# The ring of operand tiles in a pool of its own, at 4096-byte steps from byte 79,168, and the mLSTM's values in two buffers beside it

## The chip, the core and the metric

The kernel runs on one NeuronCore of a Trainium2 chip. The metric is device time in microseconds (us) of one execution, as the median of several runs. A core has a matrix engine (TensorE, PE in the rows; PEld is its weight load), VectorE (DVE), ScalarE (ACT), GpSimd (POOL) and SyncE (SP), which here issues the DMAs. The engines run on their own instruction streams and meet at semaphores. The on-chip memory SBUF has 128 partitions; an address here is a byte inside a partition, the same in all of them.

## What is computed

The reference runs two blocks of a network one after the other on 256 tokens of width 1024, in fp32. The first has two layers; each is a mixer (mLSTM, dilated attention, gates) and a gated MLP. The second block has two layers too: a windowed attention with 256 context tokens beside the 256 tokens, then a gated linear attention (GLA), each followed by an MLP of hidden width 4096. All weights are read from HBM once.

```python
def first_block(x, c, ...):
    h = layer_norm(x)
    for l in range(2):
        u = h * (1.0 + sc1) + sh1
        y = mixer(u, w_in[l], ...)          # mLSTM, attention, gates: u @ w_in and more
        h = layer_norm(DN_ALPHA * h + g1 * y, ln1_g[l], ln1_b[l])
        u = h * (1.0 + sc2) + sh2
        h = layer_norm(DN_ALPHA * h + g2 * swiglu(u, w1[l], w3[l], w2[l]), ln2_g[l], ln2_b[l])

def channel_mlp(h, w_in, w_out):            # second block
    return jnp.square(jax.nn.relu(h @ w_in)) @ w_out
```

## The kernel before

**Weights.** The weights are packed into 591 tiles of 128x1024 fp32 for the main stream, which `ahead` (L450 and after) keeps moving: SP loads `raw`, ScalarE rounds it to `wh` (L464), VectorE makes the rest `wl = raw - wh`. These tiles lie in the pool `wp`, each at 128 behind a multiple of 256 bytes. A weight tile with the matmuls that use it is called a granule; `gran` (L477) emits one. Each product is made of three TensorE passes, `mm3` (L581): activation-high by `wh`, activation-low by `wh`, activation-high by `wl`.

**Two kinds of product.** In `mm_ws` (L588) the weight slice, 128x128, is loaded as the stationary operand and the activations stream past it, 256 columns at a time (rows `mm<-uT,wh`: first the moving operand, then the stationary one). A granule of this kind has 8 slices of the contraction, k = 0 to 7, and 24 matmuls. In `mm_nat` and the "row" products of the second block the activations are stationary and 512 columns of weight stream (rows `aux<-wh,hid`).

**Where the operands lie.** Activation tiles come from rings. `t4` (L432) hands out tiles of up to 4112 bytes a partition from 27 buffers, in turn; `t2` (L429) tiles of 2048 bytes from 8. Both rings are tags of the one pool `p`. The widest `t4` tile is `v1`, the mLSTM's values with a column of ones, 4x257 fp32, 4112 bytes; the pool rounds that up to 4128. The built program puts the `t4` ring at bytes 78,720 + 4128 n, so the starts of its 27 buffers go through all eight remainders 0, 32, ..., 224 of 256, and the `t2` ring at 202,368 + 2048 n, remainder 128 each. A tile of split activations (`t4x4`, L434) holds two slices k, each with a high and a low part of 1024 bytes, so all its operands have the remainder of its buffer; a granule reads four such tiles. `mlg` (L1097), the hidden activations of the first block's MLP, is a `t2` tile and holds one slice's high and low part.

**What a ring makes wait.** The first write of a tile waits for the last access of the tile that had the buffer before. `order` of the work on each engine is fixed when the program is built: granules follow the list `PLAN`, background generators (`tick`) put other work between them, and VectorE's extra products for the modulation vectors (`ada_step`) are put where a model of TensorE's and VectorE's time (`Core`) has room. The addresses do not enter that model.

Of the kernel before, what the change touches and what calls it, by code (L numbers as in the profile page):

```python
# [9 lines left out]
F32 = mybir.dt.float32  # L10
# [298 lines left out]
class Views(list):  # L309


    def __init__(self, views, pair):
        super().__init__(views)
        self.pair = pair
# [62 lines left out]
class Kernel:  # L377
    LOAD, HI, LO, RAWS = 5, 3, 2, 4

    def __init__(self, ctx, tc, i, o):  # L380
        self.tc, self.nc, self.i, self.o = tc, Core(tc.nc), i, o
        nc = self.nc
        pool = lambda name, bufs, **k: ctx.enter_context(tc.tile_pool(name=name, bufs=bufs, **k))
        self.const = c = pool("const", 1)
        self.wp = pool("wp", 4)
        self.ps = pool("ps", 2, space=PSUM)
        self.p = pool("p", 1)
        self.cur = self.nload = self.nhi = self.nlo = 0
        self.raws, self.hi, self.W = {}, {}, {}
        self.bg, self.deferred = [], []  # L390
        self.filler = iter(())
        self.kv, self.on = [None, None], [None, None]
        self.mix_filler = [self.ctx_qkv, self.ctx_in]
        self.mlp_filler = [self.ctx_out, self.ctx_mlp]
        self.adaq, self.ada_left, self.adaraw = [], {}, {}
        self.room = -250
        self.hold = False
        self.vec = c.tile([128, i["vec"].shape[1]], F32, name="vec")
        self.ident = c.tile([128, 128], F32, name="ident")
        make_identity(tc.nc, self.ident)  # L400
        self.identr = c.tile([128, 128], F32R, name="identr")
        nc.vector.tensor_copy(out=self.identr, in_=self.ident)
        self.ones = c.tile([128, 1], F32, name="ones")
        nc.vector.memset(self.ones, 1.0)
        self.mhalf = c.tile([128, 16], F32, name="mhalf")
        nc.vector.memset(self.mhalf, -0.5)
        self.x = None
# [19 lines left out]
        return self.p.tile([128, 256], F32, tag="t1", name=name, bufs=5)  # L427

    def t2(self, name, shape=(128, 512), dt=F32):  # L429
        return self.p.tile(list(shape), dt, tag="t2", name=name, bufs=8)  # L430

    def t4(self, name, shape, dt=F32):  # L432
        return self.p.tile(list(shape), dt, tag="t4", name=name, bufs=27)

    def t4x4(self, name, n=8):

# [348 lines left out]

    def values(self):

        v1 = [self.t4("v1", (128, 4, 257)) for _ in range(2)]
        for b in range(2):
            self.nc.gpsimd.memset(v1[b][:, :, 256:257], 1.0)  # L790
        return v1
# [1011 lines left out]
    def layer2_attention(self, x, xc):  # L1803
        nc = self.nc
        cols = self.scales(0, "g_pre_mix_2", 0, 1, (0,))
        h = self.next_h(0, x, None, None, cols, lag=2)
        while not h:
            self.tick(False)
            self.fill()
        self.fill(99)  # L1810
        self.hold = False
        h = self.wait(h)
        for cb in (2, 0, 1):
            for _ in self.qkv(0, cb, h, [self.aux(), self.aux()]):
                self.tick(False)
        self.flush()

        self.on[0] = [self.t4("on", (128, 1024)) for _ in range(2)]
        oT = [None] * 8
        pools = (self.aux,) * 4 + (self.trb,)  # L1820
        left = [(0, b, hq) for hq in range(16) for b in range(2)]
        for n, u in enumerate(left):
            self.add(self.unit(pools[n % len(pools)], *u), n)
            if n % 8 == 7:
                self.add(self.o_out(0, n // 8, oT, self.trb), n + 7)
        other = self.mlp_out(1, 1, self.hid_c, self.yc, self.mmb)
        n = 0
        while self.bg:
            n += 1
            self.tick(False)  # L1830
            self.run_deferred()
            if n in (1, 2, 4, 6, 12, 18, 24, 30):
                next(other, None)
            if self.adaq and self.nc.late < self.room:
                self.ada_step()
        self.rest(other)
        gc = self.gain_cols(0, "g_post_mix_2", 2, 0)
        cols = self.scales(0, "g_pre_mlp_2", 3, 4, (0,))
        yl = [[None] * 2 for _ in range(2)]
        for hf in range(2):  # L1840
            banks = [self.aux(), self.aux()]
            for kp in range(4):
                self.gran(("awo", 0, hf, kp), self.mm_nat(kp, self.tokens(oT), banks))
                if hf == 0 and kp == 1:
                    G = self.bcast_cols(gc, "G")
            for b in range(2):
                yl[b][hf] = banks[b]
        ul = self.next_h(0, x, yl, G, cols, lag=2)
        uc = self.uc
        hc = []  # L1850
        for _ in self.mlp_in(2, 1, uc, hc):
            self.tick(False)

        ul = self.wait(ul)
        y = [self.t4("y", (128, 1024)) for _ in range(2)]
        yl = self.halves(y)
        yh = yl + self.yc
        for g in range(3):
            hid = []
            self.rest(self.mlp_in(g, 0, ul, hid))  # L1860
            if g < 2:
                self.rest(self.mlp_out(g, 0, hid, yl, self.aux))
            else:
                self.flush()
                act = lambda k, hl, b: (hid if b < 2 else hc)[k][:, hl, b % 2 * 128:(b % 2 + 1) * 128]
                self.rest(self.mlp_out(g, 2, act, yh, self.aux))
        hid, hc = [], []
        for i in range(8):
            t = self.t4("hid", (128, 2, 512), F32R)
            hid.append(t[:, :, 0:256])  # L1870
            hc.append(t[:, :, 256:512])
            ps = self.mmb()
            self.gran(("mi", 0, 24 + i, 2), self.mm_ws2(ps, [ul, uc]), lambda t=t, ps=ps: self.relu2(ps, t))
        del ul, uc
        self.uc = None
        G = [self.post_gain(0, "g_post_mlp_2", 5, st) for st in range(2)]
        cols = self.scales(1, "g_pre_mix_2", 0, 1, (0, 1))
        self.rest(self.mlp_out(3, 0, hid, yl, self.aux))
        self.h1 = [self.next_h(0, x, yl, G[0], cols, lag=2), None]
        for _ in self.mlp_out(3, 1, hc, self.yc, self.aux):  # L1880
            self.tick(False)
        self.h1[1] = self.next_h(1, xc, self.yc, G[1], cols, lag=2)
        self.h1[0] = self.wait(self.h1[0])
# [19 lines left out]
    def layer2_gla(self, x, xc):  # L1903
        nc = self.nc
# [77 lines left out]
                    yield  # L1982
            ldone.append(1)
        self.add(decay())
        kT = [self.t4("gkT", (128, 2, 512)) for _ in range(2)]
        for hd in range(4):
            ps = self.mmb()
            self.gran(("gk", hd), self.mm_ws2(ps, h), lambda hd=hd, ps=ps: nc.scalar.activation(out=kT[hd // 2][:, hd % 2], in_=ps, func=AF.Copy))
# [144 lines left out]
        for hd in range(4):  # L2133
            if hd == 1:
                self.until(lambda: ldone)
                head(0, 1)
            if hd == 3:
                head(1, 1)
            values(hd)
# [109 lines left out]
```

## Time and profile before

| | us |
|---|---|
| median of 3 runs | 2107.93 (2104.86 to 2108.47) |
| the profiled execution, its time | 2106.81 |
| its span, first to last instruction | 2105.0 |
| PE busy | 2048.7 (97%) |
| PEld busy | 1904.5 (90%) |
| DVE busy | 1587.3 (75%) |
| ACT busy | 1149.7 (55%) |

A busy PE in such a table says only that some matmul was in flight: matmuls overlap each other (a row says 283 ns for one, while the next starts some 118 ns later). What a stream of matmuls costs is read from the distance between their starts, in the timeline. The granted clock of TensorE was 1.00 (its upper level, 2.4 GHz) in nearly the whole span, 0.994 on average.

### The profile page before, as it was taken

Reading aid. Unit: us, or ns where it says so; the run is one execution under the profiler, and the core shown is the slowest. Engines: PE = TensorE matmul, PEld = TensorE weight load, DVE = VectorE, ACT = ScalarE, POOL = GpSimd, SP = SyncE. Lnnn points to the kernel's source line nnn. Section 1 sums busy time; section 2 is a strip of 40 time slices with the busy share of each in tenths; the row PEclk is TensorE's granted clock in tenths of the full one; section 3 lists DMA queues with packets and bytes.
Section 4 is the critical chain, followed back from the end, with each engine's and each line's share of the span. In section 5 each row is a group of like instructions: output and inputs, shape, how many; then the busy total and the mean of one; then the engine's idle time right before and its main releaser. Section 6 shows DMA issues by size and latency. Waiting matters only on the chain.

```text
span 2105.0 us, 38238 instructions
## 1 busy us (share of the span) xinstructions
PE 2048.7 (97%) x15176; PEld 1904.5 (90%) x15176; DVE 1587.3 (75%) x2717; ACT 1149.7 (55%) x1968; POOL 44.4 (2%) x62
## 2 busy tenths in 40 slices
PE   7999999999999999999999999999999999998998
PEld 6999998899998998998999988899998989877997
DVE  7788887698978988998899876777563485466555
ACT  5756665555545656665644455556542464545444
POOL 0000000000000000000000000000000010000000
PEclk9999999999999999999999999999999999999999
DMA  8786566588876786655589855215552352224654
GB/s 336 279 311 215 179 233 215 190 299 305 301 258 207 280 285 227 201 192 189 161 281 352 294 197 180 71 42 179 191 186 95 114 177 86 72 69 145 195 188 134
DMA packets 120884, 426.88 MB, mean 203 GB/s; under 512 B 13664, under 2 KB 18528, under 8 KB 120704
## 3 DMA queue, kind: packets, MB, share of 16 engines
q1 hardware_dynamic: 120704, 424.43, 59.1%
q8 instruction: 119, 1.95, 0.4%
q14 instruction: 61, 0.50, 0.1%
HBM read 423.33 MB, written 1.05 MB: 202 GB/s over the span
## 4 chain that ended last, share of the span: by engine, by line
PE 88%; DVE 6%; ACT 4%; issue 1%; POOL 0%; DMA 0%; DVEq 0%; POOLq 0%; SPq 0%; ACTq 0%
PE mm L338 54%; PE aux L338 28%; PE trb L338 5%; DVE wl L338 1%; ACT wh L464 1%; POOL rs L667 0%; DVE yg L338 0%; ACT xh L1460 0%; DVE mtmp L338 0%; ACT u L896 0%; DVE araw L338 0%; ACT ah L905 0%; DVE ee L338 0%; ACT u L1498 0%; DVE xh L338 0%
## 5 line engine op out<-in xcount | busy, mean ns | idle before, releaser
L338 DVE TENSOR_TENSOR wl<-raw,wh 128x1024 fp32r<-128x1024 f32 x591 | 718.9, 1221 | 165.5 <-PE aux L338 71.1
L464 ACT ACTIVATE wh<-raw 128x1024 fp32r<-128x1024 f32 x591 | 623.6, 1059 | 345.2 <-PE mm L338 121.8
L338 PE MATMUL mm<-uT,wh 128*128 128x256 f32 x3488 | 630.2, 283 | 0.0
L338 PEld LDWEIGHTS mm<-uT,wh 128*128 128x128 f32 x3488 | 535.4, 189 | 2.2 <-ACT va L807 0.4
L338 PE MATMUL mm<-uT,wl 128*128 128x256 f32 x1744 | 488.8, 280 | 0.0
L338 PE MATMUL mm<-hT,wh 128*128 128x256 f32 x1888 | 341.6, 283 | 4.0 <-ACT y L1765 2.1
L338 PEld LDWEIGHTS mm<-uT,wl 128*128 128x128 f32 x1744 | 329.1, 189 | 0.0
L338 PEld LDWEIGHTS mm<-hT,wh 128*128 128x128 f32 x1888 | 293.6, 190 | 10.7 <-ACT y L1765 2.3
L338 PE MATMUL mm<-hT,wl 128*128 128x256 f32 x944 | 265.7, 282 | 0.0
L338 DVE CUSTOM_DVE_ANT_0 araw<-araw,silu 128x1024 f32<-128x1024 f32 x192 | 233.1, 1219 | 7.4 <-DMA araw<-in_w 5.0
L338 PE MATMUL aux<-wh,hid 128*128 128x512 f32 x640 | 199.5, 393 | 0.0
L338 PEld LDWEIGHTS mm<-hT,wl 128*128 128x128 f32 x944 | 178.7, 189 | 0.0
L338 PEld LDWEIGHTS aux<-wh,hid 128*128 128x128 f32 x640 | 117.7, 188 | 24.1
L338 PE MATMUL aux<-mlg,wh 128*128 128x256 f32 x704 | 129.5, 285 | 0.0
L338 DVE TENSOR_TENSOR r<-r 128x256 f32<-128x256 f32 (+1 forms) x88 | 39.4, 448 | 117.5 <-ACT r L1898 117.4
L338 PE MATMUL aux<-wl,hid 128*128 128x512 f32 x320 | 125.4, 392 | 0.0
L338 PEld LDWEIGHTS aux<-mlg,wh 128*128 128x128 f32 x704 | 109.3, 191 | 0.0
L1898 ACT ACTIVATE r<-mm 128x256 f32<-128x256 f32 (+1 forms) x88 | 35.9, 408 | 125.7 <-PE mm L338 125.7
L338 PE MATMUL aux<-mlg,wl 128*128 128x256 f32 x352 | 99.5, 283 | 0.0
L667 POOL TENSOR_TENSOR rs<-ve,mhalf 128x1 f32<-128x1 f32 (+1 forms) x48 | 40.9, 852 | 2043.5 <-DVE ve L338 1858.4
L338 DVE CUSTOM_DVE_ANT_0 junk<-araw,silu 128x1024 bf16<-128x1024 f32 x64 | 77.9, 1217 | 0.0
L338 PE MATMUL mm<-wh,hT 128*128 128x256 f32 (+1 forms) x352 | 77.1, 316 | 0.5 <-DVE qs L338 0.5
(364 smaller groups left out, 3088.1 us busy)
## 6 DMA issues: line engine op xcount, KB each, us to landing
raw<-in_w SPq DMA_DIRECT2D x591, 512.0 KB, 3.9
araw<-in_w SPq DMA_DIRECT2D x192, 512.0 KB, 5.1
abias<-in_abias SPq DMA_DIRECT2D x32, 192.0 KB, 5.5
xc<-in_ctx SPq DMA_DIRECT2D x4, 512.0 KB, 5.9
x<-in_x SPq DMA_DIRECT2D x2, 512.0 KB, 4.2
gb<-in_ln SPq DMA_DIRECT2D x2, 512.0 KB, 6.0
out_x<-x SPq DMA_DIRECT2D x4, 256.0 KB, 2.0
mk<-in_mmask SPq DMA_DIRECT2D x1, 512.0 KB, 5.8
```

What stands on the lines that cost most here:

```text
L338: return f(*a, **k)
L464: nc.scalar.activation(out=wh, in_=self.raws[self.nhi], func=AF.Copy)
L667: nc.gpsimd.tensor_tensor(out=rs, in0=ve, in1=self.mhalf[:, 0:n], op=ALU.pow)
L1898: nc.scalar.activation(out=r[:, 0:n], in_=ps, func=AF.Relu)
```

## The change

Three pools take the place of one. `p4` holds a tile `gap` of 448 bytes and then the `t4` ring, now 25 buffers; `p2` holds the `t2` ring, still 8 buffers; `p` keeps the rest. The three pairs of tiles `v1`, the second block's `on` and `gkT` leave the `t4` ring and take turns in two buffers of a new tag `tv` in `p`. With `v1` gone the widest tile of the `t4` ring has 4096 bytes.

```diff
@@ Kernel.__init__
+        self.p4, self.p2 = pool("p4", 1), pool("p2", 1)
         self.p = pool("p", 1)
+        nc.gpsimd.memset(self.p4.tile([128, 112], F32, name="gap"), 0.0)
@@
     def t2(self, name, shape=(128, 512), dt=F32):
-        return self.p.tile(list(shape), dt, tag="t2", name=name, bufs=8)
+        return self.p2.tile(list(shape), dt, tag="t2", name=name, bufs=8)
     def t4(self, name, shape, dt=F32):
-        return self.p.tile(list(shape), dt, tag="t4", name=name, bufs=27)
+        return self.p4.tile(list(shape), dt, tag="t4", name=name, bufs=25)
+    def tv(self, name, shape):
+        return self.p.tile(list(shape), F32, tag="tv", name=name, bufs=2)
@@ values
-        v1 = [self.t4("v1", (128, 4, 257)) for _ in range(2)]
+        v1 = [self.tv("v1", (128, 4, 257)) for _ in range(2)]
@@
-        self.on[0] = [self.t4("on", (128, 1024)) for _ in range(2)]
+        self.on[0] = [self.tv("on", (128, 1024)) for _ in range(2)]
@@
-        kT = [self.t4("gkT", (128, 2, 512)) for _ in range(2)]
+        kT = [self.tv("gkT", (128, 2, 512)) for _ in range(2)]
```

In the built program the addresses become these (start of a buffer, in bytes of a partition):

| ring | before | after |
|---|---|---|
| `t4` | 78,720 + 4128 n, 27 buffers, remainders of 256: all of 0, 32, ..., 224 | 79,168 + 4096 n, 25 buffers, remainder 64 |
| `t2` | 202,368 + 2048 n, 8 buffers, remainder 128 | 181,568 + 2048 n, 8 buffers, remainder 64 |
| `tv` | in the `t4` ring | 205,024 and 209,152, remainders 224 and 0 |
| weights (`wp`), identity matrix (`const`) | remainder 128; 64 | the same |

The order of the instructions on PE, DVE, ACT and SP is the same in both programs. On POOL one instruction is added, at the start of the program. Before, POOL begins with its constants and then fills the identity matrix `ident`, the padding `pad` and the state `mst`:

```order
L2245 UNCONDITIONAL_BRANCH
masks.py:197 MEMSET ident 128x128
L690 MEMSET pad 128x520
masks.py:199 ISA
masks.py:199 AFFINE_SELECT ident<-ident 128x128
L690 MEMSET pad 128x520
```

After, at the same place:

```order
L2252 UNCONDITIONAL_BRANCH
L390 MEMSET gap 128x112
masks.py:197 MEMSET ident 128x128
L697 MEMSET pad 128x520
masks.py:199 ISA
masks.py:199 AFFINE_SELECT ident<-ident 128x128
```

The fill of `gap` stands ahead of the fill of `ident`; nothing else has moved.

## Rows read from the trace of the kernel before

**Rows 1.** The page: busy time and share by engine; then the chain's shares by engine.

```profile
PE 2048.7 (97%) x15176; PEld 1904.5 (90%) x15176; DVE 1587.3 (75%) x2717; ACT 1149.7 (55%) x1968; POOL 44.4 (2%) x62
...
PE 88%; DVE 6%; ACT 4%; issue 1%; POOL 0%; DMA 0%; DVEq 0%; POOLq 0%; SPq 0%; ACTq 0%
```

**Rows 2.** Groups by shape, PE: line, operation, out<-moving,stationary, xcount | busy, mean ns | idle before.

```profile
L338 PE MATMUL mm<-uT,wh 128*128 128x256 f32 x3488 | 630.2, 283 | 0.0
L338 PE MATMUL mm<-uT,wl 128*128 128x256 f32 x1744 | 488.8, 280 | 0.0
L338 PE MATMUL mm<-hT,wh 128*128 128x256 f32 x1888 | 341.6, 283 | 4.0 <-ACT y L1765 2.1 <-ACT r L1898 1.4 <-DVE hT L338 0.3
L338 PE MATMUL mm<-hT,wl 128*128 128x256 f32 x944 | 265.7, 282 | 0.0
...
L338 PE MATMUL aux<-mlg,wh 128*128 128x256 f32 x704 | 129.5, 285 | 0.0
...
L338 PE MATMUL mm<-mT,wh 128*128 128x256 f32 x256 | 48.9, 291 | 2.6 <-ACT mT L650 1.9 <-DVE mT L338 0.7
L338 PE MATMUL mm<-yat,wh 128*128 128x256 f32 x256 | 46.6, 283 | 0.7 <-DVE yat L338 0.3 <-ACT yat L650 0.3
...
L338 PE MATMUL mm<-ybT,wh 128*128 128x256 f32 x128 | 23.2, 283 | 0.0
```

**Rows 3.** Timeline, PE, a granule of `uT`: start us, length us, operation, xcount.

```profile
708.60 0.40 PE L338 MATMUL mm<-uT,wh 128*128 128x256 f32 x2
...
709.30 0.39 PE L338 MATMUL mm<-uT,wh 128*128 128x256 f32 x2
...
709.98 0.40 PE L338 MATMUL mm<-uT,wh 128*128 128x256 f32 x2
...
710.68 0.39 PE L338 MATMUL mm<-uT,wh 128*128 128x256 f32 x2
...
711.39 0.40 PE L338 MATMUL mm<-uT,wh 128*128 128x256 f32 x2
```

**Rows 4.** Timeline, PE, a granule of `mlg` at slices k = 3 and k = 7.

```profile
454.63 0.40 PE L338 MATMUL aux<-mlg,wh 128*128 128x256 f32 x2
...
456.07 0.40 PE L338 MATMUL aux<-mlg,wh 128*128 128x256 f32 x2
```

**Rows 5.** Timeline, PE: 512-column products, stationary at remainder 128, then at 64.

```profile
1498.56 0.62 PE L338 MATMUL aux<-wh,hid 128*128 128x512 f32 x2
...
1499.92 0.62 PE L338 MATMUL aux<-wh,hid 128*128 128x512 f32 x2
...
1583.34 0.62 PE L338 MATMUL aux<-wh,hid 128*128 128x512 f32 x2
...
1584.71 0.62 PE L338 MATMUL aux<-wh,hid 128*128 128x512 f32 x2
```

**Rows 6.** Windows: stretch, its us, busy us of each engine (instructions), PEclk, DMA share, GB/s.

```profile
421.00:474.00 53.00, 53.00 (x454) 53.00 (x453) 49.15 (x90) 28.91 (x63) 0.00 (x0) 1.00 0.89 299
...
684.00:737.00 53.00, 52.55 (x385) 49.12 (x384) 50.76 (x70) 35.21 (x46) 0.00 (x0) 1.00 0.79 280
```

**Rows 7.** Waits: engine, line, waited for: us in total, times, longest us.

```profile
PE mm L338 <- DVE wl L338: 4.0, 2, 2.4
...
POOL v L790 <- PE mm L338: 12.1, 2, 9.6
```

**Rows 8.** Timeline: the last PE reader of an `hT` tile, and VectorE's first `qT` write.

```profile
1313.16 0.39 PE L338 MATMUL aux<-wl,hT 128*128 128x512 f32 x1
...
1320.75 0.68 DVE L338 CAST qT<-trb 128x512 fp32r<-128x512 f32 x1
```

**Rows 9.** Timeline, POOL and PE, start of the program.

```profile
0.73 0.20 POOL masks.py:197 MEMSET ident<- 128x128 f32 x1 [0.29 <-POOLq L2242]
...
3.47 1.94 PE L338 MATMUL trb<-ident,silu 128*128 128x128 f32 x8 [3.47 <-DVE silu L338]
```

## The prediction

> **What bounds the kernel now.** I read the page first: PE is busy for 97% of the span and makes 88% of the chain of work that ended last [rows 1]. A busy PE need not be a fast PE, so the second view is that of the waits: those of PE are few, the longest kind between weights and PE being 4.0 us in all [rows 7]. So TensorE streams nearly all the time, and what decides is the distance from the start of one matmul to the start of the next. The third view, the groups by shape, says which matmuls there are: 256 activation columns moving past a weight slice [rows 2]. By `mm3` there is one `wl` pass to two `wh` passes, so the five families there hold 3488 + 1744 (`uT`), 1888 + 944 (`hT`), 704 + 352 (`mlg`), 256 + 128 (`mT`), 256 + 128 (`yat`), and with 128 + 64 of `ybT` that is 10,080 matmuls. At some 118 ns each they take 1190 us, over half of the span.
>
> The fourth view, the timeline of single granules, is where the change bites, because the distance depends on the remainder of the moving operand's address by 256. The granule of `uT` at 708.6 us reads four tiles of two slices, six matmuls each; in the built program these lie at the remainders 64, 64, 160 and 128. Their starts are 0.70, 0.68, 0.70 and 0.71 us apart [rows 3]: per matmul 117, 113, 117 and 118 ns, in one granule, with the same weight tile and the same engines busy beside it. `mlg`, at remainder 128 in all its granules, takes 1.44 us for twelve: 120.0 ns [rows 4].
>
> I then paired every matmul of the trace with its instruction in the program, in order, and averaged the distances below 160 ns by the remainder of the moving operand. Remainder 64: 115.5 ns (1,333 distances). 128: 119.1 (3,236). 0, 32 and 96: 118.2 (862, 1,014, 648). 160: 117.6 (1,558). 192: 117.9 (1,091). 224: 119.1 (405). The 64s are 2 to 4 ns below the others in every part of the span that has them, with VectorE busy or idle. Over the 65 granules that read the tiles of rows 3, the distances by place are 115, 120, 116, 115, 114, 114 in the first tile and 114 in all six places of the second: the first four matmuls after another remainder are slow, and then it settles at 114.
>
> **The change, part by part.** *Addresses.* All 10,080 moving operands come to remainder 64; 1,380 are there now, 8,700 elsewhere. Their mean today over all is 118.0 ns (8,700 at 118.4 and 1,380 at 115.5). For afterwards there are three values. The mean of the 64s today is 115.5, but this has entries from other remainders in it. The second tile of rows 3 gives 113.3, without any entry. A granule that enters once, as the first tile does, and then stays, costs 694 + 3 x 684 = 2,746 ns for 24, which is 114.4; granules are often parted by transposes or other matmuls, so I take this one. The term is 10,080 x (118.0 - 114.4) = 36 us saved. Its ends are 10,080 x 2.5 = 25 us and 10,080 x 4.7 = 47 us.
>
> *Products with 512 moving columns.* Here the weights move, at remainder 128 before and after, and the ring's tile is stationary. With it at 128, six starts span 1.36 us, 227 ns each; with it at 64, 1.37 us, 228 ns [rows 5]. By the pairing the means are 228.3 (887 matmuls at 128), 230.3 (240 at 64) and 232.5 to 233.8 at the other remainders (984). All come to 64: 887 x 2.0 = +1.8 us and 984 x -2.6 = -2.5 us, together -0.7. A further 384 matmuls with 256 moving weight columns and `hT` stationary have no row at 64; at the other remainders they run at 116 to 120 ns, so they are worth between -1 and +1 us, and I take 0.
>
> *The other engines.* VectorE's and ScalarE's instructions show no such dependence: for VectorE's additions of 512 elements the means are 687 to 692 ns at five remainders. The order of work on them is unchanged, so nothing is added or saved there.
>
> *Shorter ring, 25 + 2 buffers for 27.* The price could be a first write that now waits for the last reader of its buffer, with all that is queued behind it on its engine. I took the time of every instruction from the trace and asked, with the buffers of the changed program, how long after the last access of the old tile the new one is first written. The closest case in the `t4` ring is VectorE's first write of a `qT` tile at 1320.75 us, into the buffer of an `hT` tile whose last reader started at 1313.16 [rows 8]: 7 us of room; the next have 10 and 12 us. No SP load into the ring has less than 19 us, so the weight stream behind it on SP is not held. The shorter ring costs 0. The two closest cases of today, POOL's fill of `v1` that waited 12.1 us for PE [rows 7], go away, since `v1` has buffers of its own; POOL has nothing behind it that PE waits for, so this too is worth 0.
>
> *POOL's extra fill.* It stands ahead of `ident`, whose own fill of a larger tile takes 0.20 us at 0.73 us. PE first uses `ident` at 3.47 us, when VectorE's `silu` is there [rows 9]. Worth 0, covered by over 1.5 us; without the cover it would be 0.2 us.
>
> *What is late next.* With PE faster, VectorE has less time. From 421 to 474 us it is busy 49.15 of 53.00 us; PE would need 51.4 there, so it still fits. From 684 to 737 us it is busy 50.76 us, and PE would want 51.3 [rows 6]: here VectorE, at 99%, would take part of the gain. I allow 2 us for this stretch and its like.
>
> Sum: -36 - 0.7 + 2 = -35 us. The profiled execution took 2106.8 us, its span 2105.0; it would come to 2072. The median of the runs is 1.1 us above that execution, so the forecast is 2073 us.
>
> **The rivals.**
>
> *VectorE takes over.* If VectorE can't run above some 93% of its time, as in the fullest stretch but one of rows 6, then the stretches from 420 to 580 us and from 680 to 950 us gain nothing, some 430 of 2105 us, and with the lower end of the main term the gain is 25 x 0.8 = 20 us or less: 2088 to 2100. Against it: the weights' low part is ready 3 to 6 us before PE wants it in nearly all of these granules, and PE waited 4.0 us in all for `wl` [rows 7].
>
> *The address is not the cause.* Then what is faster is the place in the granule, and the time stays at 2107. The Trainium skill speaks for this rival: "SBUF — State Buffer", section "Who interferes with whom", gives PE two independent read ports, one for the moving operand and one for the weight load, and says that PE and ACT never wait on anyone. By that rule no address could change the distance, and the forecast would be 2107 us. Against the rival stand rows 3 and 4: one form of instruction at 113 and at 120 ns, and tiles of remainder 64 that are faster as first, second and fourth tile of a granule alike. So the rule does not describe these rows, and I leave the rival 4 in 100.
>
> *A run of one remainder locks at the slow end: slower than before.* In rows 4 a long run at one remainder, 128, is the slowest there is. The second matmul of the first tile above, also at 64, takes 120 ns. If 10,080 matmuls at 64 settled at 120 to 121 ns, the price would be 10,080 x 2.5 = 25 us: 2133 us. It decides from 118.0 ns on. Against it: 64 follows 64 in the second tile of rows 3, and that is where 113 ns stand. 4 in 100.
>
> *The change doesn't do what it says.* The built program has all operands at 64, so this is excluded.
>
> **How the numbers follow.** The forecast, a gain of 20 to 47 us: 82 in 100. VectorE takes over, 5 to 20 us gained: 8. Cause elsewhere, no change: 4. Slow lock: 4. More than 47 us: 2. The range goes from the lower end of the term, 2108 - 47 - 1 = 2060, to the case with the mean of today's 64s and VectorE's losses, 2108 - 25 + 5 = 2088, and a little into the first rival, 2090. A measurement of this kernel tells about 0.2%, 4 us, from no change: faster by more 0.91, within it 0.05, slower by more 0.04.
>
> **What would show it.** In the timeline of the changed kernel a granule of `mlg` from k = 3 to k = 7 should take 1.37 us where it takes 1.44, and all four tiles of a `uT` granule 0.68 to 0.70 us. PE's waits for `wl` should stay below 10 us in all, and no new wait of SP or VectorE for PE should stand at a first write into the ring. The forecast is wrong in its main term if the `mlg` granules stay at 120 ns, and in its allowance if they fall to 114 and the span does not follow.

## The result and the profile after

Below, before and after name the two kernels. The changed kernel takes 2086.87 us (median of 6 runs, 2078.74 to 2092.44); the kernel before took 2105.75 us on the same chips (6 runs, 2103.35 to 2108.47). The ratio is 0.9911, with a 95% interval of 0.9896 to 0.9925: 19 us faster. The forecast was 2073 us, 2060 to 2090. The direction is right and the time lies in the range, but the gain is little more than half of the 35 us that the sum gave.

The profiled execution of after took 2092.44 us, the slowest of the six; before's took 2106.81. So the two traces have 14.4 us between them, and the readings below account for those 14.4.

The page of after, busy time by engine and the chain's shares, as in [rows 1]:

```profile
span 2090.7 us, 38245 instructions
...
PE 2030.9 (97%) x15176; PEld 1888.9 (90%) x15176; DVE 1586.6 (76%) x2717; ACT 1149.3 (55%) x1968; POOL 45.1 (2%) x63
...
PE 87%; DVE 7%; ACT 4%; issue 1%; DMA 1%; POOL 0%; DVEq 0%; POOLq 0%; SPq 0%; ACTq 0%
```

The number of matmuls is the same, and PE is still busy for 97% and still makes nearly the whole chain. The mean length of a matmul has hardly moved either; this is the after side of [rows 2] (groups by shape, PE):

```profile
L338 PE MATMUL mm<-uT,wh 128*128 128x256 f32 x3488 | 622.3, 282 | 0.0
L338 PE MATMUL mm<-uT,wl 128*128 128x256 f32 x1744 | 487.0, 279 | 0.0
```

282 ns where there were 283: the length of one says nothing, only the distance between starts does. Those distances are of two kinds now. Here are two stretches of `uT` in after, each with the last slice of one granule and the first seven of the next (timeline, PE, start and length in us; every other slice's line of `wh`, so that six matmuls lie between two lines; all operands at remainder 64):

```profile
209.62 0.39 PE L338 MATMUL mm<-uT,wh 128*128 128x256 f32 x2
...
210.30 0.39 PE L338 MATMUL mm<-uT,wh 128*128 128x256 f32 x2
...
210.98 0.39 PE L338 MATMUL mm<-uT,wh 128*128 128x256 f32 x2
...
211.66 0.39 PE L338 MATMUL mm<-uT,wh 128*128 128x256 f32 x2
...
212.34 0.39 PE L338 MATMUL mm<-uT,wh 128*128 128x256 f32 x2
...
216.46 0.40 PE L338 MATMUL mm<-uT,wh 128*128 128x256 f32 x2
...
217.17 0.40 PE L338 MATMUL mm<-uT,wh 128*128 128x256 f32 x2
...
217.87 0.40 PE L338 MATMUL mm<-uT,wh 128*128 128x256 f32 x2
...
218.58 0.40 PE L338 MATMUL mm<-uT,wh 128*128 128x256 f32 x2
...
219.29 0.40 PE L338 MATMUL mm<-uT,wh 128*128 128x256 f32 x2
```

The first stretch steps 0.68 us for six matmuls, 113.3 ns each, four times over. The second, 7 us later, steps 0.70 to 0.71 us, 117.8 ns each, also four times over. Same shape, same remainder, same kind of weight tile. `mlg` shows the same two speeds, from slice k = 3 to k = 7, where [rows 4] had 1.44 us:

```profile
425.84 0.39 PE L338 MATMUL aux<-mlg,wh 128*128 128x256 f32 x2
...
427.20 0.39 PE L338 MATMUL aux<-mlg,wh 128*128 128x256 f32 x2
...
435.98 0.40 PE L338 MATMUL aux<-mlg,wh 128*128 128x256 f32 x2
...
437.40 0.40 PE L338 MATMUL aux<-mlg,wh 128*128 128x256 f32 x2
```

1.36 us, 113.3 ns, in the first; 1.42, 118.3 ns, in the second.

To see how many there are of each, the starts of 404 of the 420 granules (without `ybT` and a few of `mT` and `yat`) were taken from the trace and the distances averaged over places 17 to 23 of each granule. In after 136 granules have 113 or 114 ns, and are called fast below; 268 have 118, and are called slow; none lies between. By family, fast of all: `uT` 87 of 218, `hT` 23 of 118, `mlg` 5 of 44, `yat` 12 of 12, `mT` 9 of 12. In before the same count spreads over 115 to 120, with all 44 of `mlg` at 120.

The bill of the two traces:

| | before | after | worth |
|---|---|---|---|
| mean distance of the 256-column matmuls, ns | 118.03 | 116.42 | 1.61 x 10,080 = 16.2 us gained |
| mean distance of the 512-column ones, ns | 230.72 | 229.74 | 0.98 x some 2,200 = 2 us gained |
| PE's gaps beyond the stream's distance, us | 152.4 | 156.7 | 4 us lost |

16 + 2 - 4 = 14, which is what lies between the two executions. Of the gaps, part is two waits that grew (views of the waits, after): `wl`, 4.0 us in [rows 7], and one transpose:

```profile
PE mm L338 <- DVE wl L338: 4.4, 2, 2.4
...
PE trb L338 <- DVE ke L338: 2.8, 1, 2.8
```

The rest is spread over many places: the attention products `aux<-v,PT` and the transposes of `xh` take about 1 us more each, from start to start. VectorE did not become the bound: in the two stretches of [rows 6] it is busy for 49.88 and 49.70 of 53 us. PE does more matmuls in each, but in the second, with 444 for 385, that is because other work stands there by then (columns: stretch, its us, busy us of PE, PEld, DVE, ACT, POOL, clock, DMA share, GB/s):

```profile
421.00:474.00 53.00, 53.00 (x460) 53.00 (x459) 49.88 (x95) 29.92 (x66) 0.00 (x0) 1.00 0.91 317
684.00:737.00 53.00, 52.25 (x444) 50.51 (x443) 49.70 (x71) 34.67 (x47) 0.00 (x0) 1.00 0.81 284
```

### The profile page after: what moved, and what is told of

Its sections match the earlier page's. It is cut to its first block, busy times and chain, and to the rows that moved or that the text cites. A ratio compares the mean times of both kernels' runs of the same rounds, so it can differ in the third digit from the quotient of the medians.

```text
span 2090.7 us, 38245 instructions
## 1 busy us (share of the span) xinstructions
PE 2030.9 (97%) x15176; PEld 1888.9 (90%) x15176; DVE 1586.6 (76%) x2717; ACT 1149.3 (55%) x1968; POOL 45.1 (2%) x63
## 4 chain that ended last, share of the span: by engine, by line
PE 87%; DVE 7%; ACT 4%; issue 1%; DMA 1%; POOL 0%; DVEq 0%; POOLq 0%; SPq 0%; ACTq 0%
PE mm L338 54%; PE aux L338 28%; PE trb L338 5%; DVE wl L338 1%; ACT wh L471 1%; DVE yg L338 1%; POOL rs L674 0%; ACT xh L1467 0%; DVE mtmp L338 0%; DMA raw<-in_w 0%; DVE xh L338 0%; DVE x L338 0%; DVE araw L338 0%; ACT ah L912 0%; DVE ee L338 0%
## 5 line engine op out<-in xcount | busy, mean ns | idle before, releaser
L471 ACT ACTIVATE wh<-raw 128x1024 fp32r<-128x1024 f32 x591 | 623.6, 1059 | 336.2 <-PE mm L338 117.7
L338 PE MATMUL mm<-uT,wh 128*128 128x256 f32 x3488 | 622.3, 282 | 0.0
L338 PEld LDWEIGHTS aux<-wh,hid 128*128 128x128 f32 x640 | 117.7, 188 | 23.6 <-DVE hid L338 0.2
```

The source lines that it names most:

```text
L338: return f(*a, **k)
L471: nc.scalar.activation(out=wh, in_=self.raws[self.nhi], func=AF.Copy)
```

## What had to be told apart

The trace alone leaves three questions. Is it the address at all, or the new pools and the shorter ring? If the address, is it the operand's own, or its distance from the weights' address? And what decides which of the two speeds a granule gets? The theory going in: the address makes the speed; at an address 64 below the weights' remainder (also called a distance of 64 below; the distance between starts is always given in ns or us) there are two stable speeds, a granule keeps the one in which it starts, and what stands before it chooses. Some figures of after and before led to that. A granule that follows directly on another kept its speed in 143 of 143 cases when it was slow and in 49 of 50 when it was fast; of the 25 that followed a granule of `mlg`, all kept its speed too, 3 fast and 22 slow. After something else, the granules of after started like this:

| what PE did just before | fast | slow |
|---|---|---|
| transposes of `ident` | 48 | 15 |
| `aux<-wl`, a 512-column product | 5 | 29 |
| attention products `trb<-kT,qT` or `trb<-v,PT` | 1 | 31 |
| `aux<-qk` | 9 | 3 |

And in before, where tiles of all remainders mix, a run at 64 that followed a tile at 128 was fast in 86 of 86 cases.

Every kernel below computes everything that the kernel before does.

## Experiments on the address

**The pools and buffers alone.** 25 + 2 buffers and the three pools as in the change, but the `t4` ring keeps its old step of 4128 bytes, so its remainders go through all eight; `t2` stays at 128.

```diff
-        nc.gpsimd.memset(self.p4.tile([128, 112], F32, name="gap"), 0.0)
+        nc.gpsimd.memset(self.p4.tile([128, 1028], F32, tag="t4", name="wide", bufs=25)[:, 0:112], 0.0)
+        nc.gpsimd.memset(self.p2.tile([128, 56], F32, name="gap"), 0.0)
```

> The shorter ring (25 buffers), the two buffers for the mLSTM's values and the pools as in the changed kernel, but the t4 ring keeps steps of 4128 bytes (all eight remainders) and the t2 ring keeps remainder 128. Theory A (all of the gain is the distance between matmuls, set by the operands' addresses): no gain, 2102 to 2110 us, mean distance of the 256-column matmuls 118.0 ns. Rival B (part of the gain comes from the buffers, by waits that went away): the part of the 19 us that is B's, 2087 to 2100 us, with the distance unchanged at 118.0 ns.

Measured: 2109.36 us (7 runs), ratio 1.0028 [1.0016, 1.0039] to 2103.75 us of before. Its page:

```profile
span 2105.9 us, 38247 instructions
...
PE 2050.4 (97%) x15176; PEld 1906.1 (91%) x15176; DVE 1587.3 (75%) x2717; ACT 1150.4 (55%) x1968; POOL 45.2 (2%) x64
```

The mean distance is 118.26 ns, near the 118.03 of before. So nothing of the gain comes from the buffers, and the profiled spans (2105.9 and 2105.0) are nearly equal. By the medians it is 5.6 us slower. 0.23 x 10,080 = 2.3 us of that is the distance, since the buffers now stand in another mix of remainders; the other 3 us are not explained.

**All operands at remainder 128 instead of 64.** The only edit is the length of the gap; order and buffers are those of after.

```diff
-        nc.gpsimd.memset(self.p4.tile([128, 112], F32, name="gap"), 0.0)
+        nc.gpsimd.memset(self.p4.tile([128, 64], F32, name="gap"), 0.0)
```

> The changed kernel with a gap of 256 bytes instead of 448, so that both rings lie at remainder 128 as the weights do. Theory A: every granule runs as those of mlg did before the change, 120.0 ns, so 10,080 x (120.0 - 116.4) = 36 us above the changed kernel, 2123 us (2118 to 2130). Rival C (what counts is that all tiles have one remainder, whichever): 2087 us as in the changed kernel, 116.4 ns. Rival B: 2087 us.

Measured: 2118.76 us (2 runs), ratio 1.0071 [1.0051, 1.0092], 32 us above after. A granule of `hT` in it, seven slices apart (timeline, PE):

```profile
1292.34 0.40 PE L338 MATMUL mm<-hT,wh 128*128 128x256 f32 x2
...
1294.86 0.40 PE L338 MATMUL mm<-hT,wh 128*128 128x256 f32 x2
```

2.52 us for 21 matmuls: 120.0 ns. 400 of the 404 granules stand at 120, the mean is 119.84. The address is the cause, and the slow end that rows 4 showed is the steady state of operand and weights at one remainder. It came out 4 us below the expected middle of 2123 us; some 3.5 us of that come from the 512-column products, now at 228.16 ns (1.6 ns less than in after, by some 2,200).

**The weights moved as well.** Weights at remainder 192, operands at 128: the operand again stands 64 below the weights, but no longer at 64.

```diff
+        wg = pool("wg", 1)
+        nc.gpsimd.memset(wg.tile([128, 16], F32, name="wgap"), 0.0)
-        nc.gpsimd.memset(self.p4.tile([128, 112], F32, name="gap"), 0.0)
+        nc.gpsimd.memset(self.p4.tile([128, 48], F32, name="gap"), 0.0)
```

> Both rings at remainder 128, but the weight tiles moved by 64 bytes to remainder 192, so that the moving operand again lies 64 below the weights (modulo 256). Theory A1 (the remainder of the moving operand counts against that of the weight slice that is loaded meanwhile): as the changed kernel, two speeds of a granule, 113.3 and 117.7 ns, 2080 to 2095 us. Theory A2 (the remainder of the moving operand counts by itself): 120.0 ns as with all at 128, 2118 to 2130 us.

Measured: 2083.45 us (2 runs), ratio 0.9904 [0.9884, 0.9923]. Two stretches of its timeline (PE), one of two `uT` granules, one of an `hT` granule:

```profile
300.44 0.39 PE L338 MATMUL mm<-uT,wh 128*128 128x256 f32 x2
...
305.20 0.39 PE L338 MATMUL mm<-uT,wh 128*128 128x256 f32 x2
...
1259.71 0.40 PE L338 MATMUL mm<-hT,wh 128*128 128x256 f32 x2
...
1262.19 0.40 PE L338 MATMUL mm<-hT,wh 128*128 128x256 f32 x2
```

4.76 us for 42 matmuls, 113.3 ns, and 2.48 for 21, 118.1 ns: the same two speeds. What stood at 120 ns at remainder 128 with the weights at 128 now stands at 113 or 118. So the remainder of the operand alone does not decide; the distance between operand and weights, modulo 256, does: after, this kernel and the one with all at 128 agree on it. Here 260 granules were fast and 138 slow.

**Other remainders.** The gap at 72, 104 and 120 elements puts all operands at 160, 32 and 96, with the weights at 128.

> Both rings at remainder 160, 32 above the weights. Theory A: no granule at 113.3 ns; uniform granules at the mean of the tiles at 160 before the change, 117.6 ns, so 10,080 x 1.2 = 12 us above the changed kernel, 2099 us (2092 to 2108). If a granule's first matmuls decide between two speeds at every remainder, there are granules at two speeds here too.

> Both rings at remainder 32, 96 below the weights. Theory A1: uniform granules at about the mean of the tiles at 32 before the change, 118 ns, so 2100 to 2110 us, and no granule at 113.3 ns.

> Both rings at remainder 96, 32 below the weights. Theory A1: uniform granules at about 118 ns, as the tiles at 96 before the change, 2100 to 2110 us. If the two speeds come from how the two streams fall against each other, this remainder may hold two speeds as well.

Measured, one run each: 2104.89, 2108.95 and 2112.64 us, beside 2103.75, 2105.13 and 2105.13 of before. The mean distances are 116.95, 118.22 and 118.32 ns; no granule holds 113 in any of them. At 160 the granules lie at 116 to 118 in one broad group. None of them has the two speeds of 64, and the 512-column products take 233 ns in all three, so no other remainder of those tried comes near. The first two times lie in the expected ranges; that at 96 is 2.6 us above its range, with the mean distance at the expected 118 ns.

**Only the low weights moved.** `wh` stays at 128, `wl` goes to 192, and the operands stay at 64: the pool put in ahead of the ring moves its start by 64 bytes, so that the ring is at 64 with a gap of 128 bytes. Two of three matmuls then keep the distance of after, 64 below their weights, and each third one, with `wl`, stands 128 away from them.

```diff
+        self.wlp = pool("wlp", 1)
+        nc.gpsimd.memset(self.wlp.tile([128, 16], F32, name="wgap"), 0.0)
-        nc.gpsimd.memset(self.p4.tile([128, 112], F32, name="gap"), 0.0)
+        nc.gpsimd.memset(self.p4.tile([128, 32], F32, name="gap"), 0.0)
-                wl = self.wp.tile([128, 1024], F32R, tag="wl", name="wl", bufs=3)
+                wl = self.wlp.tile([128, 1024], F32R, tag="wl", name="wl", bufs=3)
```

> The changed kernel, but the low weights wl lie at remainder 192 instead of 128, so that every third matmul's weight load stands 128 from the activations instead of 64. Theory D: the two speeds belong to one relation held through a whole granule; with the relation changed in every third matmul neither can be held, and all granules have one speed between 113 and 119 ns, with no split. Rival E: the split stays, at 113.3 and 117.7 ns.

Measured: 2111.29 us (one run, beside one of 2105.13 of before). All granules have means of 118 or 119 ns, without a split; inside a granule the distances wander from 114 to 124 and no pattern settles. An `hT` granule of it (timeline, PE), 2.48 us for 21 matmuls:

```profile
1282.21 0.40 PE L338 MATMUL mm<-hT,wh 128*128 128x256 f32 x2
...
1284.69 0.40 PE L338 MATMUL mm<-hT,wh 128*128 128x256 f32 x2
```

So the two steady speeds are gone, although two of three matmuls stand at the distance that has them in after: in this mix, the only one tried, nothing is left of the gain. The mean of all is 118.19 ns, where before has 118.03.

## Experiments on what chooses the speed

**The first tile of each `uT` granule at 128.** If a run at 64 that follows a tile at 128 is always fast, as it was in before, then one tile at 128 ahead of three at 64 should make the granules fast that are slow in after, though it has a slow tile of its own.

```diff
+        self.pk, self.p4, self.p2 = pool("pk", 1), pool("p4", 1), pool("p2", 1)
-        return self.p4.tile(list(shape), dt, tag="t4", name=name, bufs=25)
+        return self.p4.tile(list(shape), dt, tag="t4", name=name, bufs=24)
+    def tk(self, name):
+        return self.pk.tile([128, 2, 2, 256], F32R, tag="tk", name=name, bufs=1)
-        t = [self.t4(name, (128, 2, 2, 256), F32R) for _ in range(n // 2)]
+        t = [self.tk(name) if name == "uT" and j == 0 else self.t4(name, (128, 2, 2, 256), F32R) for j in range(n // 2)]
```

> The changed kernel, but the first of the four tiles of every uT group lies at remainder 128, in a buffer of its own (24 buffers in the t4 ring). Theory D (at remainder 64 a granule holds one of two speeds, 113.3 or 117.7 ns, and which one is set by what runs ahead of its first matmul; entry from a matmul at 128 leads to the fast one, as 86 of 86 entries did in the kernel before): the uT granules outside mlg run their first tile at 118 to 120 ns and are at 113.3 ns in the last two tiles in at least 90 of 100, where it is about 40 of 100 in the changed kernel. Rival E (the speed is drawn anew and does not depend on the entry): still about 40 of 100. The time moves by under 5 us either way (2080 to 2095 us), since the slow first tile takes back what the others gain.

> e5 again, timed: 2080 to 2090 us, some 2 us below the changed kernel; uT granules fast in 190 to 218 of 218.

Measured: 2085.07 us at first (one run), and in the repeat 2083.89 (4 runs), ratio 0.9908 [0.9894, 0.9923]. `uT` is fast in 202 and in 200 of its 218 granules, where after had 87. One of them in the first of the two executions (timeline, PE):

```profile
301.34 0.40 PE L338 MATMUL mm<-uT,wh 128*128 128x256 f32 x2
...
302.06 0.39 PE L338 MATMUL mm<-uT,wh 128*128 128x256 f32 x2
...
303.76 0.39 PE L338 MATMUL mm<-uT,wh 128*128 128x256 f32 x2
```

From 301.34 run the second slice of the tile at 128 and the first slice behind it: 0.72 us for six, 120 ns a matmul. The next fifteen matmuls take 1.70 us, 113.3 ns. In `hT`, where nothing was edited, 23 granules are fast in the first execution, as in after. What stands before a run does choose its speed. The time gained against after is small, because a pinned granule, that is one whose first tile stands at 128, pays for this tile.

**The same for `hT`.** `t4` with 22 buffers, one buffer at 128 for the first tile of `uT` and two for that of `hT`.

```diff
-        return self.p4.tile(list(shape), dt, tag="t4", name=name, bufs=25)
+        return self.p4.tile(list(shape), dt, tag="t4", name=name, bufs=22)
+    def tk(self, name):
+        return self.pk.tile([128, 2, 2, 256], F32R, tag="tk" + name, name=name, bufs={"uT": 1, "hT": 2}[name])
-            t = [self.t4("hT", (128, 2, 2, 256), F32R) for _ in range(4)]
+            t = [self.tk("hT")] + [self.t4("hT", (128, 2, 2, 256), F32R) for _ in range(3)]
```

> As e5, and the first of the four tiles of the hT groups that one helper makes for the second block lies at remainder 128 too (two buffers of its own, 22 in the t4 ring). Theory D: the granules of these hT tiles, too, are at 113.3 ns in their last two tiles in at least 90 of 100 (22 of 118 in the changed kernel); each wins some 50 ns, 6 us together, so 2077 to 2083 us if the shorter ring costs nothing. Rival F (the ring of 22 buffers holds something up): above 2087 us with fast granules all the same.

Measured: 2081.53 us (4 runs, 2078.50 to 2083.17), ratio 0.9893 [0.9878, 0.9908]. `hT` is fast in 116 of 117 granules. Two that follow each other (timeline, PE):

```profile
1262.09 0.40 PE L338 MATMUL mm<-hT,wh 128*128 128x256 f32 x2
...
1262.80 0.39 PE L338 MATMUL mm<-hT,wh 128*128 128x256 f32 x2
...
1264.50 0.39 PE L338 MATMUL mm<-hT,wh 128*128 128x256 f32 x2
1264.85 0.40 PE L338 MATMUL mm<-hT,wh 128*128 128x256 f32 x2
...
1265.56 0.39 PE L338 MATMUL mm<-hT,wh 128*128 128x256 f32 x2
...
1266.92 0.39 PE L338 MATMUL mm<-hT,wh 128*128 128x256 f32 x2
```

0.71 us for the second slice of the tile at 128 and the slice behind it, then 1.70 us for fifteen matmuls (113.3 ns); in the next granule 0.71 again, then 1.36 for twelve (113.3). By its median this version is 5 us below the changed kernel and 22 below the one before; the intervals of the two ratios overlap, so that it beats the changed kernel is likely, not certain. With nearly all of `uT` and `hT` pinned, the mean is 115.29 ns: the tile at 128 and the first slice behind it run at some 118.2 ns, 9 of 24 matmuls, and 113.4 x 15/24 + 118.2 x 9/24 = 115.2. The 114.4 of the prediction is not reached even so.

**Weights at 192, operands at 128, first `uT` tile 64 above the others, at 192; and the weights' shift again.** The first joins the edit of the weights with that of the first tile, the second is the kernel with the weights moved once more.

> e3 and e5 together: weights at 192, rings at 128, the first uT tile at 192, the remainder of the weights. Theory D with A1: the uT granules are fast in their last two tiles in at least 90 of 100, as in e5; e3 had 159 of 218 without this, so the gain over e3 is small, 0 to 4 us, and the slow first tile may eat it: 2076 to 2086 us.

> e3 again, with more rounds, to see how far its time and its share of fast granules are its own or those of one execution. Theory D: the share of fast granules is set by what runs ahead of each, and the same program has about the same share again, 230 to 290 of 404, and 2078 to 2088 us. If the share is drawn anew in each execution, it may come out anywhere between 130 and 270, with the time up to 12 us higher.

Measured: 2081.22 us (4 runs, 2080.67 to 2081.95), ratio 0.9894 [0.9878, 0.9911], with `uT` fast in 217 of 218; and 2087.73 us (4 runs, 2086.30 to 2090.70), ratio 0.9926 [0.9911, 0.9941], with 209 fast granules and 193 slow. The first says that the effect of the first tile, too, goes by the distance to the weights. The two kernels ran side by side and differ only in that tile and its buffer; no run of the one overlaps with those of the other, so the pinned tile is worth some 6 us here.

The second missed its expectation: the same program had 260 fast granules the time before, `mlg` 27 of 44 then and 5 now. In the two executions of the `uT` edit `hT` likewise had 23 and 63. So part of the choice differs from one execution of a program to another. Each pair ran on two chips, with one trace on each, so whether the chip or the single execution makes the difference is not shown. The time goes with the count: the three profiled executions in which all operands stand 64 below the weights took 2092.44, 2086.84 and 2080.36 us, with 136, 209 and 260 fast granules. The spread of the times is no proof: it is 13.7 us over 6 runs of after and 5.1 us over 6 of before, but 4.4 us over 4 of the kernel with the weights moved, 5.4 and 4.7 us over 4 each of the two kernels with first tiles at 128, and 1.3 us over 4 of the kernel that has both edits.

## Why the prediction was half right

**The bound, and the address as the cause: right.** PE streams throughout, and what decides is the distance between starts. The rival that the address is not the cause falls with the kernel at 128: the same order and buffers, 32 us more. (The counts of distances that the prediction gives by remainder add up to 10,147, more than the 10,080 matmuls, so some other matmuls are among them, at 128 above all; paired again, the means move by 0.1 ns at most.) This also tells against the rule on the two read ports that the prediction took from the Trainium skill ("SBUF — State Buffer", section "Who interferes with whom"): here two operands of one kind of matmul give 113, 118 or 120 ns by where they lie to each other.

**The term of the 256-column matmuls: its step failed.** The prediction took 114.4 ns from "a granule that enters once, as the first tile does, and then stays". Measured are 116.42 in the profiled execution, a gain of 16 us for 36, and the 20 us missing are (116.4 - 114.4) x 10,080. That execution was the slowest of six. At the same distance, the kernel with the weights moved had 115.07 in its trace, 30 us by the same count: the term was too large by 6 to 20 us, and none of the kernels reached 114.4. The failure is in the sample. It was the second tile of the granules of [rows 3], whose four tiles lie at 64, 64, 160 and 128: there the run at 64 always begins behind the tile at 128 of the granule before. That entry is fast in 86 of 86 cases, so the sample could show nothing but 113 and 114, and I read it as the property of remainder 64. In a run of one remainder no such entry exists, and in the profiled execution two thirds of the granules hold 118. The sign was in the trace of before: runs at 64 that came from 224 were fast in 33 and slow in 5, those from transposes fast in 10 and slow in 4. The mean of 115.5 over all 64s hid it, as a mean of two speeds does. For the same reason the lower end of the term, 25 us, was no bound: it came from a mix of entries that the change took away.

**The time in the range: in part luck.** The range ends at 2090 us by an allowance for VectorE and a piece of the rival in which VectorE takes over, and neither came. The gain of 19 us lies just outside the 20 to 47 us to which the prediction gave 82 in 100, and inside the 5 to 20 us that it gave to VectorE with 8 in 100, without VectorE being the cause. The slowest of the six runs, 2092.44 us, lies outside the range.

**The slow lock: half right as a mechanism.** The rival had long runs settle at 120 to 121 ns and lose 25 us. They do settle, and most at a slow speed, but that speed is 117.7 ns, just below the mean of before, so that it costs nothing, and a third of the granules of that execution holds 113.3. At 128 the rival's speed is met, 119.84 ns, and the kernel takes 2118.76 us, 15 us more than before.

**512 columns.** The prediction had 0.7 us gained, and some 2 us were; all come to 229.7 ns, near the 228 of [rows 5]. The 384 matmuls with `hT` stationary, put at 0 within 1 us, took 48.5 us from start to start in before and 49.4 in after. A pair after it (timeline, PE, after; seven slices apart):

```profile
1476.36 0.62 PE L338 MATMUL aux<-wh,hid 128*128 128x512 f32 x2
...
1481.17 0.62 PE L338 MATMUL aux<-wh,hid 128*128 128x512 f32 x2
```

4.81 us for 21 products, 229 ns.

**VectorE, allowance 2 us.** The 4 us of gaps are twice the allowance, but a TensorE that outruns VectorE is not their cause, and in the stretch that was named VectorE went down to 49.70 us. Counted from start to start, what grew are PE's matmuls other than the two kinds above, transposes and attention products most of all: 341.9 us in before and 345.7 in after, but 345.4 too in the kernel at 128, whose stream is slower than that of before, and 342.5 in the one with the buffers alone. What lengthens them stays open. The rival that VectorE takes over did not come: PE waits 4.4 us for `wl`, and 4.1 us in the version with pinned `uT` and `hT`, which is 5 us faster still.

**Shorter ring and POOL's fill, 0.** POOL's wait at `v1` [rows 7] is gone, no new wait at a first write into the ring stands in the view of waits, and the buffers alone gained nothing. That they cost some 3 us, as the medians of that kernel say beyond its distance, is neither shown by a wait nor excluded.

**What stays open.** Why a distance of 64 has two speeds, and what in the transposes or products ahead chooses one of them, is not settled; only the choice by a tile at equal remainder was put to the test. In before, runs at 64 behind 224 were mostly fast as well, so an equal remainder may not be needed. And why one program has different counts of fast granules in two executions is not known.

## What to carry to other kernels

When a stream of matmuls bounds a kernel, measure the distance between starts by the address of the moving operand against that of the weights, and look at the distribution by granule, not at the mean: two stable speeds give a mean that no granule has. Before a steady value is taken from a sample of a mixed trace, see what always stands ahead of the sample and whether the change takes that away. And one profiled execution shows one set of counts, which need not be that of the median run. A change of placement can be tried at the cost of one gap tile, in a kernel whose order stays the same.

## What the runs showed of the hardware

For 256-column matmuls with 128x128 weights at the upper clock (mean granted clock 0.99 in these runs): 113.3 or 117.7 ns where the operand's address is 64 below the weights' modulo 256, held through granule after granule with few exceptions, and chosen in part by what ran before; 118.2 ns, without the two speeds, where each third matmul stood 128 away instead; 120.0 ns where the two are equal; 117 to 118.3 ns at the other distances tried, without a split. For 512-column products with the ring's tile stationary: 228.2 ns with all at 128, 229.7 at 64, 233 at 32, 96 and 160. With two speeds open, one program had 260 fast granules in one execution and 209 in another, at 2080.36 and 2086.84 us.
